# Chunk pairs of the modulated input padded by 32 bytes, in a two-layer decoder trunk

## The chip, the cores and the metric

The kernel runs on one core of a Trainium2 chip. The metric is the time of one execution on the device, in microseconds; less is better. The time before is the median of three executions.

## What is computed

Two layers of a decoder over one sequence of 256 tokens with 2048 features, in f32. Layer 0 mixes tokens with a forgetting attention of 16 heads, layer 1 with a sliding-window attention of 32 query heads; each mixer is followed by a gated feed-forward network whose up-projection passes a causal convolution of width 3. Cut to what matters:

```python
for i in range(DEPTH):                                   # DEPTH = 2
    sh1, sc1, g1, sh2, sc2, g2 = split(silu(c) @ ada_w[i] + ada_b[i], 6)
    h = x * (1 + sc1) + sh1
    y = fox_attention(h, ...) if i == 0 else swa_attention(h, ...)
    x = layer_norm(ALPHA * x + (1 + g1) * y)
    h = x * (1 + sc2) + sh2
    u = causal_conv3(h @ w_up)                           # 2048 -> 2 * 5632
    y = (silu(u[..., :5632]) * u[..., 5632:]) @ w_down
    x = layer_norm(ALPHA * x + (1 + g2) * y)
```

## The kernel before, in words

**Split products.** Every large product runs as float32r matmuls on operands that are split into a high and a low part. A weight tile `w` of 128 partitions x 2 x 512 comes by DMA from SyncE's queue. `stream` has ScalarE copy its high part into `wh` (L264) and VectorE put the rest into `wl` (L275). Of each product, the terms high x high, high x low and low x high are added in PSUM.

**The modulated input.** `h = x * (1 + scale) + shift`, transposed, stands in one tile `hHL`: 16 chunks of 128 features, each with 256 f32 numbers of the high part (`hH`) and then 256 of the low part (`hL`), 2048 bytes a chunk in each partition. `mod_pair` writes two chunks at a time.

**Who multiplies it.** Four kinds of product read the operands; all matmuls are issued through the helper at L75, so the profile tells them apart by tiles. The operand named as stationary is put into the array by a weight load, a separate instruction; the moving one streams through.

- `u_mm`, tile `us`, the up-projections: a piece of `wh` is stationary, and `hH` and `hL` together stream as 512 columns; then a piece of `wl` is stationary and `hH` streams as 256 columns.
- `w_mm`, tile `ws`, the query and key projections of layer 0: the same operands in three matmuls of 256 columns.
- `x_mm` with `hstat`, tile `xs<-..,hHL`: a piece of `hHL` is stationary and 512 columns of `wh` or `wl` stream. The value projections of layer 0, all projections into layer 1's attention, and the last four of the 16 chunks of both output projections, whose attention output `o_tile` puts into `hHL`.
- `x_mm` with `gT` or `oT`: the same with stationary pieces in buffers of the pool `gp` (down-projections, the other 12 chunks of the output projections).

**Order.** `stream` puts weight tiles into a list, `settle` takes them off it; attention heads, evictions and the adaLN vectors are generators that advance between tiles. The adaLN weights come by the same queue, and VectorE multiplies and adds them (L404).

**Where the tiles lie.** In each partition `hHL` begins at byte 27,904, the four buffers of `wh` at 119,776 and every 4096 on, those of `wl` at 136,160, those of the pool `gp` at 152,544 and every 2048 on. Pieces of `wh`, `wl`, `gT`, `oT` and `hHL` that a weight load reads are 512 bytes long and begin at multiples of 512 from these. So every moving operand lies at one offset from every stationary one, modulo 512 bytes: `hHL` lies 288 behind the weights' pieces where it moves, the weights lie 224 behind `hHL`'s pieces where `hHL` is stationary (512 - 288), and 0 behind pieces in `gp`. The last tile ends at byte 229,280 of 229,376, so there are 96 bytes to spare; the first 4096 are a scratch for DMAs that GpSimd issues (biases, the convolution's weights, the `ada_b` rows).

Of the kernel before, what the change touches and what calls it, by code (L numbers as in the profile page):

```python
# [11 lines left out]
F32R = mybir.dt.float32r  # L12
# [5 lines left out]
P = 128  # L18
D = 2048
S = 256  # L20
NT = S // P
KC = D // P
# [19 lines left out]
def hybrid_trunk(ctx: ExitStack, tc: tile.TileContext, a: dict, out: bass.AP):  # L42
    nc = tc.nc
# [4 lines left out]
    cst = ctx.enter_context(tc.tile_pool(name="cst", bufs=1))  # L48
# [431 lines left out]
            ada_step()  # L480


    hHL = cst.tile([P, KC, 2, S], F32R, name="hHL")
    hH, hL = hHL[:, :, 0, :], hHL[:, :, 1, :]

    def mod_turn(k, n=1):

# [670 lines left out]
    for t in range(NT):  # L1158
        mu, rs, _ = moments[t]
        for d in range(D // 512):  # L1160
            c = slice(d * 512, (d + 1) * 512)
# [29 lines left out]
```

## Time and profile before

| what | us |
|---|---|
| median of three executions | 2254.76 (2251.33 to 2254.91) |
| the profiled execution, its own time | 2256.46 |
| its span, first to last instruction | 2254.7 |
| TensorE matmuls busy | 2203.7 (98%) |
| weight loads busy | 1908.6 (85%) |
| VectorE busy | 1847.5 (82%) |
| ScalarE busy | 1209.7 (54%) |
| GpSimd busy | 22.8 (1%) |
| 5632 matmuls `us`, busy | 983.7 + 790.4 |

Matmuls overlap in the trace: one starts while the one before is still shown as running. So the sum of their durations is not the time they take; that is read from the distance between starts. A weight load is shown beside the matmul before the one that it is for.

### The profile page before, as it was taken

To read this page: it belongs to the slowest core of one execution; us is meant where nothing else is said; L and a number is where in the kernel's file an instruction comes from. 1 tells how busy PE (TensorE), PEld (TensorE's weight loads), DVE (VectorE), ACT (ScalarE), POOL (GpSimd) and SP (SyncE) were. 2 spreads that over 40 slices of the span, in tenths; PEclk is the share of its full clock that TensorE was granted. 3 is DMA by queue.
4 is the path that set the end of the run, shared out by engine and by line. 5 is a ranking of instruction groups with operands and counts; after the bars stand their busy time and mean duration, and the time that the engine had idled before them with its cause. 6 is when DMAs were issued, how large, how long until landed. Compare 5 with 4: busy or idle time off the path is not lost. (4 is left out here: it accounts for less than half of the span.)

```text
span 2254.7 us, 33120 instructions
## 1 busy us (share of the span) xinstructions
PE 2203.7 (98%) x12087; PEld 1908.6 (85%) x12087; DVE 1847.5 (82%) x2626; ACT 1209.7 (54%) x2009; POOL 22.8 (1%) x52
## 2 busy tenths in 40 slices
PE   6999999999999999999999999999999999999997
PEld 5999888788888888888887788788888888888886
DVE  6879999979989978799888899769988655676766
ACT  3435655455555543655634588746555533555542
POOL 0000000000000000000000000000000000000000
PEclk9999999999999999999999999999999999999999
DMA  9999999958978989889887777557887555565553
GB/s 336 371 336 364 349 357 325 329 200 298 327 266 296 315 299 339 272 277 319 280 309 284 244 246 243 206 185 262 289 270 256 190 192 195 189 193 189 188 195 112
DMA packets 274228, 602.66 MB, mean 267 GB/s; under 512 B 21062, under 2 KB 29960, under 8 KB 273552
## 3 DMA queue, kind: packets, MB, share of 16 engines
q1 hardware_dynamic: 273008, 595.85, 76.5%
q0 software_dynamic: 1056, 4.69, 0.6%
q8 instruction: 94, 1.54, 0.3%
q14 instruction: 70, 0.57, 0.1%
HBM read 598.37 MB, written 2.10 MB: 266 GB/s over the span
## 5 line engine op out<-in xcount | busy, mean ns | idle before, releaser
L264 ACT CAST wh<-w 128x1024 fp32r<-128x1024 f32 x728 | 763.8, 1051 | 806.4 <-PE us L75 284.5
L275 DVE TENSOR_TENSOR wl<-w,wh 128x1024 fp32r<-128x1024 f32 x728 | 887.2, 1223 | 297.0 <-ACT wh L264 285.1
L75 PE MATMUL us<-hHL,wh 128*128 128x512 f32 x2816 | 983.7, 393 | 0.0
L75 PE MATMUL us<-hHL,wl 128*128 128x256 f32 x2816 | 790.4, 282 | 3.0 <-DVE wl L275 3.0
L75 PEld LDWEIGHTS us<-hHL,wh 128*128 128x128 f32 x2816 | 528.9, 188 | 112.0 <-issue 2.5
L75 PEld LDWEIGHTS us<-hHL,wl 128*128 128x128 f32 x2816 | 533.0, 189 | 8.4 <-DVE wl L275 4.3
L75 PE MATMUL xs<-wh,gT 128*128 128x512 f32 x1408 | 435.5, 390 | 0.0
L75 PEld LDWEIGHTS xs<-wh,gT 128*128 128x128 f32 x1408 | 264.3, 188 | 54.6
L75 PE MATMUL xs<-wl,gT 128*128 128x512 f32 x704 | 273.9, 389 | 0.0
L75 PE MATMUL xs<-wh,hHL 128*128 128x512 f32 x704 | 237.6, 403 | 0.1
L404 DVE SCALAR_TENSOR_TENSOR acc<-wa,cact,acc 128x1024 f32<-128x1024 f32 x180 | 228.8, 1280 | 0.0
L75 PE MATMUL ws<-hHL,wh 128*128 128x256 f32 x1024 | 191.3, 289 | 4.4 <-ACT hHL L84 2.1
L75 PEld LDWEIGHTS ws<-hHL,wh 128*128 128x128 f32 x1024 | 163.1, 196 | 6.9 <-ACT hHL L84 2.3
L404 DVE SCALAR_TENSOR_TENSOR acc<-wa,cactp,acc 128x1024 f32<-128x1024 f32 x128 | 162.6, 1281 | 0.0
L75 PEld LDWEIGHTS xs<-wh,hHL 128*128 128x128 f32 x704 | 131.5, 189 | 29.4 <-issue 1.0
L75 PEld LDWEIGHTS xs<-wl,gT 128*128 128x128 f32 x704 | 132.2, 188 | 27.3
L75 PE MATMUL ws<-hHL,wl 128*128 128x256 f32 x512 | 144.7, 290 | 2.2 <-DVE wl L275 2.2
L75 PE MATMUL xs<-wl,hHL 128*128 128x512 f32 x352 | 140.6, 400 | 1.6 <-DVE wl L275 1.5
L75 PE MATMUL xs<-wh,oT 128*128 128x512 f32 x384 | 124.6, 394 | 0.8 <-ACT wh L264 0.7
L1075 ACT ACTIVATE u<-us,ccol 128x256 f32<-128x256 f32 x176 | 98.0, 561 | 39.6 <-DVE us L1073 39.5
L75 PEld LDWEIGHTS ws<-hHL,wl 128*128 128x128 f32 x512 | 99.5, 197 | 2.8 <-DVE wl L275 2.8
L1076 DVE SCALAR_TENSOR_TENSOR u<-us,ccol,u 128x255 f32<-128x255 f32 x176 | 83.6, 480 | 13.2 <-ACT u L1075 12.9
(222 smaller groups left out, 1761.2 us busy)
## 6 DMA issues: line engine op xcount, KB each, us to landing
w<-in_ffn_w_up_dram SPq DMA_DIRECT2D x352, 512.0 KB, 4.6
wa<-in_ada_w_dram SPq DMA_DIRECT2D x320, 512.0 KB, 5.4
w<-in_ffn_w_down_dram SPq DMA_DIRECT2D x176, 512.0 KB, 4.1
w<-in_fox_w_in_dram SPq DMA_DIRECT2D x96, 512.0 KB, 7.0
wo<-in_ada_w_dram SPq DMA_DIRECT2D x48, 512.0 KB, 8.4
w<-in_swa_w_in_dram SPq DMA_DIRECT2D x40, 512.0 KB, 5.0
w<-in_fox_w_o_dram SPq DMA_DIRECT2D x32, 512.0 KB, 6.2
w<-in_swa_w_o_dram SPq DMA_DIRECT2D x32, 512.0 KB, 4.7
```

Of the source, the lines that this page charges most:

```text
L75: return nc.tensor.matmul(o, lhsT, rhs, start=start, stop=stop, **kw)
L264: pin(nc.scalar.copy(h, w), False)
L275: pin(nc.vector.tensor_tensor(l, w, f32(h), op=ALU.subtract), behind[0] > 0)
L404: pin(nc.vector.scalar_tensor_tensor(ac, wo, (cactp if row else cact)[:, k:k + 1], ac, op0=ALU.mult, op1=ALU.add), True)
L1075: nc.scalar.activation(u, pf, AF.Identity, bias=cw(CW, f), scale=cw(2, f))
L1076: nc.vector.scalar_tensor_tensor(u[:, 1:], pf[:, :S - 1], cw(1, f), u[:, 1:], op0=ALU.mult, op1=ALU.add)
```

## The change

The tile `hHL` becomes eight chunk pairs of 4 x 256 numbers with 8 unused numbers (32 bytes) behind each, 256 bytes longer in all. A class `Chunks` stands for the former three views and finds pair and chunk. The scratch of dynamic transfers is 2048 instead of 4096 bytes per partition, without which the longer tile would not fit.

```diff
-    hHL = cst.tile([P, KC, 2, S], F32R, name="hHL")
-    hH, hL = hHL[:, :, 0, :], hHL[:, :, 1, :]
+    hpad = cst.tile([P, KC // 2, 4 * S + 8], F32R, name="hHL")[:, :, :4 * S].rearrange("p j (i a s) -> p j i a s", i=2, a=2)
+
+    class Chunks:
+
+        def __init__(self, a):
+            self.a = a
+
+        def __getitem__(self, key):
+            _, k, *c = key
+            j, i = (k.start // 2, slice(0, 2)) if isinstance(k, slice) else (k // 2, k % 2)
+            return hpad[(slice(None), j, i, self.a, *c)]
+
+    hHL, hH, hL = Chunks(slice(0, 2)), Chunks(0), Chunks(1)
...
-    nc = _bacc.Bacc("TRN2", target_bir_lowering=False, num_devices=1, dynamic_dma_scratch_size=4096)
+    nc = _bacc.Bacc("TRN2", target_bir_lowering=False, num_devices=1, dynamic_dma_scratch_size=2048)
```

On each of the five engines the instructions stand in the same order as before, with the same shapes and the same waits; what differs is addresses. Tiles up to `hHL`'s start move down by 2048 bytes, those behind it by 1792. With j the number of the chunk pair, 0 to 7, `hHL` as moving operand now lies 32 + 32j bytes behind the weights' pieces modulo 512 (32, 64, ... 256, where it was 288), and the weights as moving operand lie 512 - 32 - 32j behind `hHL`'s pieces (480, 448, ... 256, where it was 224). Against pieces in `gp` they stay at 0.

## The prediction

> **What bounds the kernel now.** I read the page first. Its engine and clock rows say that TensorE is the bound nearly throughout:
>
> ```profile
> span 2254.7 us, 33120 instructions
> PE 2203.7 (98%) x12087; PEld 1908.6 (85%) x12087; DVE 1847.5 (82%) x2626; ACT 1209.7 (54%) x2009; POOL 22.8 (1%) x52
> PEclk9999999999999999999999999999999999999999
> ```
>
> The groups say which matmuls carry it, and that they hardly wait: the last column is idle time ahead of a group, and it is at most a few us in a thousand.
>
> ```profile
> L75 PE MATMUL us<-hHL,wh 128*128 128x512 f32 x2816 | 983.7, 393 | 0.0
> L75 PE MATMUL us<-hHL,wl 128*128 128x256 f32 x2816 | 790.4, 282 | 3.0 <-DVE wl L275 3.0
> L75 PE MATMUL xs<-wh,hHL 128*128 128x512 f32 x704 | 237.6, 403 | 0.1
> L75 PE MATMUL xs<-wl,hHL 128*128 128x512 f32 x352 | 140.6, 400 | 1.6 <-DVE wl L275 1.5
> L75 PE MATMUL ws<-hHL,wh 128*128 128x256 f32 x1024 | 191.3, 289 | 4.4 <-ACT hHL L84 2.1 <-ACT wh L264 1.3 <-ACT hHL L503 1.0
> L75 PE MATMUL ws<-hHL,wl 128*128 128x256 f32 x512 | 144.7, 290 | 2.2 <-DVE wl L275 2.2
> ```
>
> So 2816 pairs of `us`, 704 + 352 = 1056 `xs` with `hHL` stationary and 1024 + 512 = 1536 `ws` touch the tile that changes. Since nothing is added, removed or reordered, only the pace of these matmuls can change, and the pace is the distance between starts. I therefore read the timeline, TensorE alone, in stretches without a break.
>
> ```profile
> 1455.24 0.39 PE L75 MATMUL xs<-wl,oT 128*128 128x512 f32 x1
> ...
> 1469.52 0.39 PE L75 MATMUL xs<-wl,oT 128*128 128x512 f32 x1
> 1469.75 0.40 PE L75 MATMUL xs<-wh,oT 128*128 128x512 f32 x1
> 1469.98 0.39 PE L75 MATMUL xs<-wh,hHL 128*128 128x512 f32 x1
> 1470.21 0.39 PE L75 MATMUL xs<-wl,hHL 128*128 128x512 f32 x1
> 1470.44 0.63 PE L75 MATMUL xs<-wh,hHL 128*128 128x512 f32 x2
> ...
> 1475.11 0.40 PE L75 MATMUL xs<-wl,hHL 128*128 128x512 f32 x1
> 1475.34 0.40 PE L75 MATMUL xs<-wh,hHL 128*128 128x512 f32 x1
> 1475.58 0.39 PE L75 MATMUL xs<-wh,oT 128*128 128x512 f32 x1
> ```
>
> This is one output projection that goes over from stationary pieces in `gp` to pieces in `hHL` and back. The moving operand, the length and the engines around it are the same; only the address of the loaded piece differs. From 1455.24 to 1469.52 there are 21 rounds of three matmuls, 14.28/63 = 226.7 ns each. From 1470.21 to 1475.11 there are 7 rounds, 4.90/21 = 233.3 ns. So where the weight load reads relative to the stream costs 6.6 ns a matmul here: offset 0 is a cheap place, offset 224 a dear one. The two other kinds:
>
> ```profile
> 286.92 0.28 PE L75 MATMUL ws<-hHL,wl 128*128 128x256 f32 x1
> 287.04 0.40 PE L75 MATMUL ws<-hHL,wh 128*128 128x256 f32 x2
> ...
> 289.37 0.28 PE L75 MATMUL ws<-hHL,wl 128*128 128x256 f32 x1
> 599.70 0.39 PE L75 MATMUL us<-hHL,wh 128*128 128x512 f32 x1
> 599.93 0.28 PE L75 MATMUL us<-hHL,wl 128*128 128x256 f32 x1
> ...
> 605.94 0.39 PE L75 MATMUL us<-hHL,wh 128*128 128x512 f32 x1
> ```
>
> `ws`: 7 rounds of three, 2.45/21 = 116.7 ns for 256 columns. `us`: 18 pairs, 6.24/18 = 346.7 ns a pair. Both lie at offset 288. A pair at the cheapest rows would take 226.7 + 116.7 = 343.4. For a dear pair I take 233.3 and, for the 256 columns that no row shows dear, 116.7 plus half of 6.6, together 353.3. The pair now stands a third of the way from the cheap to the dear end.
>
> **The Trainium skill against this.** TensorE: Matmul & The Clock Gate, section Step-by-step: what each phase is for, says that the array has two independent read ports, and that "Loading the next tile's weights doesn't steal SBUF read bandwidth from the running matmul." By that rule the sum would be zero; the trace does not agree, 226.7 against 233.3 ns with only the loaded piece's address changed. The same page, section Back-to-back issue gap, gives 512/2.4 + 2.5 = 216 ns for 512 columns and 109 for 256; an estimate by it is that a change which took all interference away would save 2816 x (347 - 325) = 62 us in `us` alone, and no row here reaches that pace in these products.
>
> **The change part by part.** The cost of a load is taken as a function of the offset, moving minus stationary, modulo 512. The rows give it at 0 (cheap), 224 (dear) and 288 (a third of the way). For a new offset I take the nearest of these; that is a choice, because three points don't show a curve.
>
> *us.* The new offsets are 32, 64, ... 256 for the eight chunk pairs, each with an eighth of the matmuls. 32, 64 and 96 lie nearest to 0; I take no gain there, because no 256-column row is cheaper than now (bound: 343.4, a gain of 3.3). 128, 160, 192 and 224 lie nearest to 224: +6.6 each. 256 lies midway between 224 and 288: +3.3. Mean (4 x 6.6 + 3.3)/8 = 3.7 ns, times 2816: **+10.5 us**. Bounds: all cheap, -9.3; all dear, +18.6.
>
> *xs with hHL.* 480, 448 and 416 lie nearest to 512, that is 0: -6.6. 384, 352, 320 and 288 lie nearest to 288, a third of the way up: -4.4. 256 is midway: -2.2. Mean -(19.8 + 17.6 + 2.2)/8 = -5.0 ns, times 1056: **-5.3 us**. Bounds -7.0 and 0.
>
> *ws.* +3.3 at four offsets and +1.7 at one, mean 1.9 ns, times 1536 = 2.9 us. This stage has a second bound beside TensorE:
>
> ```profile
> 200.00:300.00 100.00, 97.12 (x728) 91.10 (x728) 92.44 (x144) 59.08 (x127) 5.85 (x12) 1.00 0.98 346
> 600.00:640.00 40.00, 40.00 (x233) 35.48 (x232) 38.72 (x55) 23.41 (x36) 0.00 (x0) 1.00 0.91 321
> 1950.00:2000.00 50.00, 50.00 (x291) 44.34 (x290) 34.75 (x53) 28.30 (x46) 0.00 (x0) 1.00 0.60 190
> ```
>
> These are stretches with the busy time of PE, PEld, DVE, ACT and POOL, granted clock, DMA share and GB/s. With DMA at 0.98 the queues take part of what TensorE loses, so I count half: **+1.4 us** (bounds 0 and +5.1). In the up-projections TensorE is busy all the time in both layers (40.00 of 40, 50.00 of 50), so there a loss counts in full; a gain in layer 0 would soon meet VectorE, 38.72 of 40 busy, which is what would be late next.
>
> *The padding itself.* Chunks are written by the same instructions with the same shapes, so nothing is taken for it; a slower write would be hidden behind the matmuls of the pair before.
>
> *The scratch.* GpSimd issues few transfers, and is idle 99% of the time. One is not far from the path: an `ada_b` row issued between the two moments of a layer norm.
>
> ```profile
> 472.28 0.57 POOL L642 TENSOR_TENSOR rs<-mv,mhalf 128x1 f32<-128x1 f32 x1 [211.50 <-DVE mv L641]
> 476.09 0.60 POOL L392 DMA_DIRECT2D acc<-in_ada_b_dram  x1 [3.24 <-PE sm L75]
> 476.71 0.57 POOL L642 TENSOR_TENSOR rs<-mv,mhalf 128x1 f32<-128x1 f32 x1
> acc<-in_ada_b_dram POOLq DMA_DIRECT2D x4, 1024.0 KB, 6.2
> ```
>
> Issuing takes 0.60 us of GpSimd. If it still fits into the scratch, it costs nothing.
>
> **The sum.** 10.5 - 5.3 + 1.4 = +6.6 us. The profiled execution took 2256.46 us, of which 2254.7 is span; it would take 2263.1. The median of the runs lies 1.7 us below that execution, so the forecast is 2254.76 + 6.6 = 2261 us. About 0.2%, 4.5 us, is what a measurement of this kernel can tell from no change.
>
> **The rivals.**
>
> *Alignment decides, not distance (faster).* The bytes modulo 64 may be what matters. The weights and the buffers of `gp` begin 32 bytes past a multiple of 64, `hHL` at a multiple: every cheap row has both operands in the same place, every other row has them 32 apart. The padding puts the four odd chunk pairs where the weights are. Then half of `xs` falls to 226.7, 528 x 6.6 = 3.5 us, and half of the `us` pairs to 343.4, 1408 x 3.3 = 4.6 us; `ws` stays. Together -8.1 us: 2247. For it speaks that it, too, explains all rows; against it that `ws` at 116.7 and `us` at 346.7 hardly show the handicap that `xs` shows. It decides from the point where fewer than about a third of the `us` loads become dear. A stronger form has every new offset cheap: -9.3 - 7.0 = -16.3, 2238.
>
> *Nothing happens (same).* While a load reads its 512 bytes, the stream runs on over more bytes than that, so that every offset modulo 512 could be met in every load, and 226.7 against 233.3 would come from something else in the place of `hHL`. Then the pace stays: 2255. This is also where the rule of the two ports ends. Against it: the pace is constant over long stretches, and differs by tile alone.
>
> *All new offsets are dear (slower still).* +18.6 + 5.1 = 23.7: 2278.
>
> *The scratch is too small (slower).* If half of it doesn't hold the descriptors of an `ada_b` row, GpSimd waits in L392 until part of the transfer has landed, with the second `rs` (L642) queued behind it; the normalisation and TensorE wait for that. Price: up to the 6.2 us of a landing, at the one layer norm shown and the like one of layer 1: up to 12 us, 2267 without any change of pace. For it speaks only the place; GpSimd had issued nothing for 200 us before.
>
> **How the numbers follow.** The forecast has 0.38, all dear 0.08, the scratch 0.03: slower 0.49. Nothing happens: same 0.18. Alignment 0.25 and all cheap 0.08: faster 0.33. The three points don't fix a curve, which is why the forecast has less than half. The range must take in both ends of the unknown curve, 2238 and 2278, with some us for what the runs scatter: 2236 to 2282.
>
> **What the profile after would show.** If I am right, the `us` pairs have two paces that change with the chunk pair: about 347 ns in the pairs 0 to 2, about 353 in the pairs 3 to 6; `xs` with `hHL` falls to 227 to 229 except in the last pair; `oT` and `gT` stay at 226.7; L392 stays at 0.6 us. Alternating cheap and dear pairs, even against odd, would speak for alignment. One pace of 346.7 in all pairs would say that the offset modulo 512 is not the cause. A `us` pace under 343 anywhere would say that my cheap end is not the end.

## The result, and the profile after

The median went from 2254.84 us (four runs, 2251.33 to 2255.42) to 2265.36 us (four runs, 2262.47 to 2265.58): 10.5 us slower, ratio 1.0047 with a 95% interval of 1.003 to 1.0064. The forecast was 6.6 us slower, 2261.

The page of the changed kernel, the rows that answer to those of before:

```profile
span 2263.2 us, 33120 instructions
PE 2212.6 (98%) x12087; PEld 1906.7 (84%) x12087; DVE 1848.3 (82%) x2626; ACT 1210.4 (53%) x2009; POOL 22.9 (1%) x52
L75 PE MATMUL us<-hHL,wh 128*128 128x512 f32 x2816 | 993.8, 397 | 0.0
L75 PE MATMUL us<-hHL,wl 128*128 128x256 f32 x2816 | 787.6, 281 | 2.9 <-DVE wl L275 2.9
L75 PE MATMUL xs<-wh,hHL 128*128 128x512 f32 x704 | 236.1, 401 | 0.1
L75 PE MATMUL ws<-hHL,wh 128*128 128x256 f32 x1024 | 192.7, 290 | 4.4 <-ACT hHL L84 2.1
```

The same instructions, no new wait, and the idle column as small as before. TensorE alone is longer busy, by 8.9 us, while VectorE and ScalarE stay within a microsecond. The group that grew is `us` beside `wh`, by 10.1 us.

Where it lies shows in the timeline of TensorE. These are the first matmuls of each chunk pair in one undisturbed up-projection (columns: start, duration, both in us). Between one row and the next stand eight `us` pairs:

```profile
1961.46 0.40 PE L75 MATMUL us<-hHL,wh 128*128 128x512 f32 x1
...
1964.24 0.39 PE L75 MATMUL us<-hHL,wh 128*128 128x512 f32 x1
...
1967.04 0.40 PE L75 MATMUL us<-hHL,wh 128*128 128x512 f32 x1
...
1969.84 0.39 PE L75 MATMUL us<-hHL,wh 128*128 128x512 f32 x1
...
1972.65 0.40 PE L75 MATMUL us<-hHL,wh 128*128 128x512 f32 x1
...
1975.43 0.39 PE L75 MATMUL us<-hHL,wh 128*128 128x512 f32 x1
...
1978.25 0.39 PE L75 MATMUL us<-hHL,wh 128*128 128x512 f32 x1
...
1981.06 0.39 PE L75 MATMUL us<-hHL,wh 128*128 128x512 f32 x1
...
1983.89 0.40 PE L75 MATMUL us<-hHL,wh 128*128 128x512 f32 x1
```

Before, every pair took 346.6 ns in the median, whatever its chunk. Now each chunk pair has a pace of its own, and keeps it from block to block. The medians over some 40 passes of each chunk pair, worked out from all starts of the trace, are 347.8, 350.5, 350.1, 350.4, 347.9, 352.2, 351.6 and 353.5 ns for the pairs 0 to 7. Their mean is 350.5, so 3.9 ns more, times 2816 pairs: 10.9 us. All eight are slower than before.

`xs` with `hHL` stationary, the last four chunks of an output projection, 24 matmuls:

```profile
1493.63 0.39 PE L75 MATMUL xs<-wh,hHL 128*128 128x512 f32 x1
...
1498.98 0.39 PE L75 MATMUL xs<-wh,hHL 128*128 128x512 f32 x1
```

5.35/23 = 232.6 ns, against 233.0 before (5.36 us for the like 23 from 1469.98 to 1475.34): hardly the fall that was forecast. The same four chunks for the 512 output columns before these fall further:

```profile
1471.79 0.39 PE L75 MATMUL xs<-wh,hHL 128*128 128x512 f32 x1
...
1477.08 0.39 PE L75 MATMUL xs<-wh,hHL 128*128 128x512 f32 x1
```

5.29/23 = 230.0 ns. Both stretches have the same offsets; what differs is the order of their matmuls.

### The profile page after: what moved, and what is told of

The parts are those of the page before. It is cut to its first block, busy times and chain, and to the rows that moved or that the text cites. A ratio compares the mean times of both kernels' runs of the same rounds, so it can differ in the third digit from the quotient of the medians.

```text
span 2263.2 us, 33120 instructions
## 1 busy us (share of the span) xinstructions
PE 2212.6 (98%) x12087; PEld 1906.7 (84%) x12087; DVE 1848.3 (82%) x2626; ACT 1210.4 (53%) x2009; POOL 22.9 (1%) x52
## 5 line engine op out<-in xcount | busy, mean ns | idle before, releaser
L75 PE MATMUL us<-hHL,wh 128*128 128x512 f32 x2816 | 993.8, 397 | 0.0
```

Source lines behind the costliest of these rows:

```text
L75: return nc.tensor.matmul(o, lhsT, rhs, start=start, stop=stop, **kw)
```

## The experiments

Each run is compared with runs of the kernel before on the same chip. "Halved" is the kernel before with the scratch of 2048 bytes; offsets are the moving operand's place behind the loaded piece.

**1. The scratch alone.**

```diff
-    nc = _bacc.Bacc(..., dynamic_dma_scratch_size=4096)
+    nc = _bacc.Bacc(..., dynamic_dma_scratch_size=2048)
```

> The kernel before with half the scratch alone: all tiles move down by 2048 bytes, no offset between operands changes (hHL 288 behind the weights everywhere). Theory (the pace of a matmul follows from the offset of the moving operand to the piece being loaded, modulo 512 bytes): no change, 2254.8 us within 2, us pairs at 346.7 ns. Rival, the scratch or the absolute place of the tiles costs the time: some 10 us more, 2265, and L392 on GpSimd longer than 0.6 us.

2254.92 against 2254.53 us, ratio 1.0008 (0.9999 to 1.0017): no change. GpSimd's issue of an `ada_b` row stands between the two `rs` as before and takes as long:

```profile
473.74 0.60 POOL L392 DMA_DIRECT2D acc<-in_ada_b_dram  x1 [3.24 <-PE sm L75]
474.36 0.57 POOL L642 TENSOR_TENSOR rs<-mv,mhalf 128x1 f32<-128x1 f32 x1
```

So neither the scratch nor the move of all tiles costs anything that these runs can see.

**2. Padding that changes no offset.** The changed kernel, with a longer pad:

```diff
-    hpad = cst.tile([P, KC // 2, 4 * S + 8], F32R, name="hHL")...
+    hpad = cst.tile([P, KC // 2, 4 * S + 64], F32R, name="hHL")...
```

> The changed kernel with 256 instead of 32 unused bytes behind each chunk pair: the same class of views, the same half scratch, chunk pairs still apart, but every pair 32 behind the weights modulo 256, as in the kernel before. Theory: the whole loss goes, 2255 within 3, us pairs at 346.5 ns, xs with hHL at 233. Rival, the padding or the scratch costs in itself, whatever the offsets: 2265.

2254.78 against 2256.36 us, ratio 0.9993 (0.9983 to 1.0003): the whole loss is gone, with the pads, the views and the small scratch still there. A whole up-projection block, 64 pairs:

```profile
1976.24 0.39 PE L75 MATMUL us<-hHL,wh 128*128 128x512 f32 x1
...
1998.42 0.39 PE L75 MATMUL us<-hHL,wh 128*128 128x512 f32 x1
```

22.18/64 = 346.6 ns, one pace. The offsets are the cause, not the padding.

**3. One offset for all chunks, 32 and 256.** The halved kernel with 256, or 32, unused bytes behind the old tile:

```diff
-    hHL = cst.tile([P, KC, 2, S], F32R, name="hHL")
+    hHL = cst.tile([P, KC * 2 * S + n], F32R, name="hHL")[:, :KC * 2 * S].rearrange(...)   # n = 64 or 8
```

> The old layout of hHL with 256 unused bytes behind it: hHL lies 32 behind the weights in all chunks, as chunk pair 0 of the changed kernel does. Theory: the pace of that pair everywhere, about 347 ns a us pair, 233 an xs with hHL: 2816 x 0.5 = 1.4 us more, 2256. Rival, the mixture of offsets costs (going from one to the next): as before, 2255, so this run alone does not part the two; rival, the shift of the weights by 1792 instead of 2048 bytes: 2265.

> The old layout with 32 unused bytes behind it: 256 behind in all chunks, as chunk pair 7 of the changed kernel, and the weights at a multiple of 64 bytes as hHL is. Theory: the pace of pair 7 everywhere, about 352 ns a us pair (+5.4 x 2816 = 15 us), 228.3 an xs with hHL (-5 x 1056 = -5 us), ws 121 (+4.5 x 1536 = 7, some of it hidden): 2269 to 2272, more than the changed kernel. Rival, the mixture costs: 2255. Rival, equal alignment modulo 64 is what makes it cheap: 2247 or less.

Offset 32: 2254.01 against 2254.53, ratio 0.9996 (0.9988 to 1.0005), the pace of before (median 346.6 ns; pair 0 of the changed kernel, at the same offset beside others, has 347.8). It also clears the shift of the weights by 1792 bytes. Offset 256: 2264.69 against 2254.53, ratio 1.0048 (1.0035 to 1.006). One uniform dear offset loses as much as the mixture of eight; a mixture is not needed. The alignment rival, by which this run should have been the fastest, falls. The expected 2269 to 2272 was too high. Over distances between starts below 300 ns (longer ones hold a wait or other work), `us` cost 13.0 us where 15 were expected, and `ws` 2.3 where 7 were, some of it hidden. Why `us` fell short is in the trace. Two blocks of 64 pairs of the same kernel:

```profile
597.58 0.39 PE L75 MATMUL us<-hHL,wh 128*128 128x512 f32 x1
...
619.77 0.39 PE L75 MATMUL us<-hHL,wh 128*128 128x512 f32 x1
...
1982.03 0.40 PE L75 MATMUL us<-hHL,wh 128*128 128x512 f32 x1
...
2004.64 0.40 PE L75 MATMUL us<-hHL,wh 128*128 128x512 f32 x1
```

22.19/64 = 346.7 ns in the first half of layer 0's up-projection, 22.61/64 = 353.3 in layer 1, at the same offsets. At this offset there are two paces; the trace stays in one for some 200 us at a time, and the changes that were followed up lie where other matmuls come between. `xs` with `hHL` gains here:

```profile
1491.66 0.39 PE L75 MATMUL xs<-wh,hHL 128*128 128x512 f32 x1
...
1496.87 0.40 PE L75 MATMUL xs<-wh,hHL 128*128 128x512 f32 x1
```

5.21/23 = 226.5 ns, the pace that `gT` has at offset 0. So modulo 256 one and the same offset, 0, is cheap for `xs` and dear for `us`, as 32 is cheap for `us` and dear for `xs` (233.1 ns in pair 6 of the changed kernel).

The run also speaks against the place of a tile by itself, without the other operand. The weights and `gp` begin 32 bytes further on here, modulo 256, than in the changed kernel. Yet that kernel's pair 7, at the same offset as all pairs here, has 353.5 ns against the 353.3 above, and `gT`, moved together with the weights, keeps its 226.8 ns.

**4. The other half of the circle.** The changed kernel with 256 unused bytes more behind the tile:

```diff
-    hpad = cst.tile([P, KC // 2, 4 * S + 8], ...)[:, :, :4 * S]...
+    hpad = cst.tile([P, KC // 2 * (4 * S + 8) + 64], ...)[:, :KC // 2 * (4 * S + 8)]...
```

> The changed kernel with 256 more unused bytes behind hHL, so that the eight chunk pairs lie 288, 320, ... 512 behind the weights: the other half of the circle. Theory: pair 0 (288) has the pace of before, 346.7 ns in us and 233 in xs with hHL; pair 7 (512, that is 0) has 226.7 in xs; the pairs between have paces of their own, from 343 to 353, not those of the changed kernel. Sum between 2245 and 2270. Rival, the mixture costs: 2265, with the same paces as in the changed kernel pair by pair.

2264.26 against 2254.53, ratio 1.0048 (1.0034 to 1.0062). The paces are those of the changed kernel, chunk pair by chunk pair: 347.8, 350.5, 350.1, 350.4, 347.9, 352.2, 351.6 and 353.5 ns as medians. The last pair, offset 512:

```profile
2001.26 0.39 PE L75 MATMUL us<-hHL,wh 128*128 128x512 f32 x1
...
2004.09 0.40 PE L75 MATMUL us<-hHL,wh 128*128 128x512 f32 x1
```

2.83/8 = 353.8, as pair 7 at offset 256 in the changed kernel (2.83/8). Here the mixture rival expected the right paces and the theory the wrong ones. Read with the two runs before, which exclude the mixture as the cause, it says that the offset counts modulo 256: 288 is 32, 512 is 256. The run of 2 agrees: its pairs lie at 288 and 32 in turn, and all have one pace.

**5. Other tiles at the dear place.** The halved kernel with 32 unused bytes ahead of the pool `gp`:

```diff
             l = hl.tile([P, 2, WB], F32R, tag="wl", name="wl")
+            hl.tile([P, 8], F32, tag="gap", bufs=1, name="gap")
```

> The layout of before with the pool gp (gT, oT) moved by 32 bytes: wh and wl, where they stream, lie 224 instead of 0 behind the pieces in gp, the place that hHL's pieces had; hHL and the weights stay as they were. Theory (offset modulo 256 between stream and loaded pieces, whatever the tiles): xs with gT goes from 226.6 to 233 ns, with oT alike, us stays at 346.5; (2112 + 576) x 6.5 = 17 us more, 2271. Rival, hHL is dear for a reason of its own (its place, who writes it): 2254.

2268.96 against 2256.23, ratio 1.0058 (1.0042 to 1.0075). The down-projections, which the change never touched, go from the first of these stretches (before) to the second, 576 matmuls in a row each:

```profile
1779.92 0.39 PE L75 MATMUL xs<-wh,gT 128*128 128x512 f32 x1
...
1910.27 0.39 PE L75 MATMUL xs<-wh,gT 128*128 128x512 f32 x1
```

```profile
1785.76 0.40 PE L75 MATMUL xs<-wh,gT 128*128 128x512 f32 x1
...
1919.92 0.40 PE L75 MATMUL xs<-wh,gT 128*128 128x512 f32 x1
```

130.35/575 = 226.7 ns became 134.16/575 = 233.3, the pace of `hHL`'s pieces to a tenth. So nothing about `hHL` itself is dear; the offset is. The loss was 12.7 us, not 17. By distances below 300 ns, `gT` lost 13.7 us and `oT` 2.9, together what was expected; the time shows 4 us less than that, and why was not followed up.

**6. Which piece counts.** As in 5, with a gap of 32 bytes ahead of `wl` instead, and 224 behind it, so that `hHL` lies 32 behind `wh` and 0 behind `wl`, modulo 256:

> The layout of before, but the buffers of wl moved by 32 bytes against those of wh (and the pool gp put back to 0 behind wh). So hHL lies 32 behind wh and 0 behind wl. Theory, what counts is the piece loaded while a matmul streams: the 512 columns of us, beside which wl is loaded, go from 228 to 234 ns, the 256 columns, beside which wh is loaded, stay at 118; 2816 x 4 to 6 = 11 to 17 us; where wl streams beside a load of gT (704) some 6 ns more, 4 us; together 2268 to 2276. Rival, what counts is the piece already in the array: the 512 columns stay at 228 and the 256 columns fall to 116 or 117, 3 to 6 us less in us, 4 more in gT: 2250 to 2256.

2266.82 against 2253.5, ratio 1.0057 (1.004 to 1.0074). The time is just under what the first reading expected (2268 to 2276), but for another reason. The `us` pairs don't slow down (first fence, 64 pairs: 22.19/64 = 346.7 ns), and `gT` slows down as a whole, though only `wl`, a third of the streams, changed its place (576 matmuls, 134.15/575 = 233.3):

```profile
1961.90 0.39 PE L75 MATMUL us<-hHL,wh 128*128 128x512 f32 x1
...
1984.09 0.39 PE L75 MATMUL us<-hHL,wh 128*128 128x512 f32 x1
```

```profile
1783.14 0.39 PE L75 MATMUL xs<-wh,gT 128*128 128x512 f32 x1
...
1917.29 0.39 PE L75 MATMUL xs<-wh,gT 128*128 128x512 f32 x1
```

Both readings fall: the first on `us`, the second on `gT`. A matmul's pace doesn't follow from its own stream and one piece; neighbours take part. The `us` pairs even gain in parts of this run, at the same offsets; a block of 64 pairs in layer 1's first half:

```profile
1597.53 0.39 PE L75 MATMUL us<-hHL,wh 128*128 128x512 f32 x1
...
1619.58 0.39 PE L75 MATMUL us<-hHL,wh 128*128 128x512 f32 x1
```

22.05/64 = 344.5 ns, so here too there are two paces. In all, `us` gains 2.1 us by distances below 300 ns.

**7. The order of the streams.** The kernel of 6, and the halved kernel as control, with `x_mm` in another order:

```diff
             for i in range(2):
                 xh, xl = stat(kc + i, t)
                 mm(ps[t], xh, h[:, i, :], start=kc + i == first)
-                mm(ps[t], xh, l[:, i, :])
-                mm(ps[t], xl, h[:, i, :], stop=kc + i == last)
+                mm(ps[t], xl, h[:, i, :])
+            for i in range(2):
+                mm(ps[t], stat(kc + i, t)[0], l[:, i, :], stop=kc + i == last)
```

> The run with wl moved by 32 bytes, with the matmuls of x_mm in another order: of two chunks first the four that stream wh, then the two that stream wl, so that the stream goes over from wh to wl and back once in six matmuls instead of twice. There all three matmuls of a round with gT had become slower (231 to 236 ns for 226.6), though only wl's stream had changed its place. If the going over from one offset to another is what costs: about half of the 13.6 us that gT lost, xs with gT at some 230 ns, 2260. If a third of the streams at a dear place sets the pace of all: no difference from that run, 233 ns, 2266. If each stream pays for itself (which that run spoke against): the same sum, with the four wh at 226.6.

> The control to the run before it: the same order of x_mm with wl in its old place. Both readings: xs with gT at 226.6 ns, 2254.

Each ran once: 2265.66 and 2257.5 us. In the first, the stretch with `gT` takes 132.67/574 = 231.1 ns:

```profile
1784.55 1.09 PE L75 MATMUL xs<-wh,gT 128*128 128x512 f32 x4
...
1917.22 0.63 PE L75 MATMUL xs<-wl,gT 128*128 128x512 f32 x2
```

The control stays at 226.7 by the starts of its trace. With half as many changes from one stream to the other, two thirds of the loss remain (4.4 of 6.6 ns). That is between the two readings and settles neither. How one matmul bears on the next stays open.

**8. Finer steps.** The changed kernel moved by 16 bytes, and one with 2 instead of 8 numbers of padding (8 bytes) from offset 0 on; each ran once. Offsets are modulo 256.

> The changed kernel with all of hHL moved by 16 bytes: the eight chunk pairs lie at 48, 80, ... 240 and 16 behind the weights modulo 256, between the offsets seen so far. Theory: each pair has a pace of its own between 343 and 353 ns in us; near the changed kernel's time, 2260 to 2268. If whole multiples of 32 are what matters (a word that straddles a line), all pairs are dearer than any seen, over 352.

> Padding of 8 bytes a chunk pair: the pairs lie at 0, 8, ... 56 behind the weights modulo 256. Theory: pair 0 at about 351 ns in us and pair 4 (32) at about 347, as seen at these offsets, and the others between; tells whether there is a place cheaper than 32 near it. If only the 16-byte line counts, pairs 0 and 1 agree, 2 and 3, and so on.

2263.12 and 2265.03 us. Offsets 48, 80, ... 240 and 16 have medians from 347.9 to 352.0 ns a pair, so whole multiples of 32 are nothing special. In steps of 8 bytes from 0 the medians are 353.0, 353.6, 348.4, 356.8, 347.2, 348.4, 346.5 and 347.0. The first matmuls of the pairs at 16, 24 and 32, eight `us` pairs apart:

```profile
1966.69 0.40 PE L75 MATMUL us<-hHL,wh 128*128 128x512 f32 x1
...
1969.47 0.39 PE L75 MATMUL us<-hHL,wh 128*128 128x512 f32 x1
...
1972.33 0.39 PE L75 MATMUL us<-hHL,wh 128*128 128x512 f32 x1
```

2.78/8 = 347.5 ns at 16 and 2.86/8 = 357.5 at 24. Places 8 bytes apart differ by 8 to 10 ns here, which speaks against 16 bytes as the unit. In these two runs no place is cheaper than 346.5, and 24 bytes is the dearest seen. But the offset does not fix a pace to the nanosecond: 48 has 349.0 in the first run and 346.5 in the second, between other neighbours.

**9. A version from what was learnt.** Two views of one tile, 32 bytes apart, so that `hHL` lies at 32 where it moves and at 0 where it is stationary (layer 1's projections, the output projections):

```diff
+    hraw = cst.tile([P, KC * 2 * S + 8], F32R, name="hHL")
+    hviews = [hraw[:, o:o + KC * 2 * S].rearrange("p (k a s) -> p k a s", a=2, s=S) for o in (0, 8)]
...
```

> One tile with 32 bytes more and two views of it, 32 bytes apart: where hHL moves (us, ws) and for layer 0's value projection it lies 32 behind the weights modulo 256, the cheap place of before; for layer 1's projections and the four chunks of both output projections that are stationary pieces in hHL, it lies at 0, where the run with 256 for all showed xs at 228.5 ns instead of 233. Theory (an offset modulo 256 for each kind of product): 672 x 4.4 = 3 us less than before, 2251.5, us pairs at 346.5 as before. Rival, the pace of xs in that run came from something else than its own offset: 2254.5.

2251.94 against 2253.5, ratio 0.9994 (0.9984 to 1.0004). The pace is what was expected, 24 matmuls of an output projection:

```profile
1485.68 0.39 PE L75 MATMUL xs<-wh,hHL 128*128 128x512 f32 x1
...
1490.89 0.40 PE L75 MATMUL xs<-wh,hHL 128*128 128x512 f32 x1
```

5.21/23 = 226.5 ns for 233, and the `us` pairs keep theirs. By distances below 300 ns `xs` with `hHL` gains 3.0 us in all, as expected. The gain of 1.6 us in the time, against 3 expected, is inside what the runs scatter, so this version is not shown to be faster than the kernel before.

## Why the prediction was right, and where not

**The bound.** TensorE's pace was the only thing that changed: same instructions, no new wait, and it stayed busy throughout in the up-projections (50.00 of the 50 us from 1950 to 2000, before and after).

**us.** Forecast +10.5 us, measured 2816 x 3.9 = +10.9 by the medians. The sum was right and its parts were not. The pairs 0 to 2 were to stay at 347 and the pairs 3 to 6 to go to 353; in fact the pairs 1 and 2 lost 3.9 and 3.5 ns, pair 4 only 1.3, and pair 7, taken at half, lost most, 6.9. The nearest of three rows is no guide to a curve that jumps within 8 bytes, and two of the three rows were those of `xs`, which has another curve: offset 0, its cheap place, is a dear one for `us`. What carried the sum was one observation: `us` stood near its cheap end, so that most other places had to be dearer. The finer runs bear it out: in them no place is cheaper than 346.5. That wrong parts came to the sum within half a us is luck.

**xs with hHL.** Forecast -5.3 us, which is 5.0 ns a matmul. Over distances below 300 ns the mean went from 233.2 to 232.0 ns, so -1.3 us. The step that failed is the offset modulo 512. It counts modulo 256, so 480 is 224, the dear row itself, where the forecast took it for near 0; and 256 is 0. The five projections of layer 1 show it, with means over each chunk pair: 233.4, 233.3 and 233.6 ns in the pairs 0 to 2, which were to fall most; 229.9 in pair 5 and 229.1 in pair 7; 232.2 to 233.1 in the others.

**ws.** Forecast +1.4 us after halving; by the same distances 124.1 and 125.2 ns, +1.6 us. But in runs that leave the offset of `ws` as it was, this mean lies between 122.1 (run of 9) and 124.3 (run of 1), so that the term is not clear of what the stage scatters.

**The sum.** By the same distances `us` has +10.4, and all three +10.4 - 1.3 + 1.6 = +10.7, against 10.5 in the medians and 8.5 in the two spans. The forecast of 6.6 fell short mostly by the gain of `xs` that did not come. So the direction and the bearer of the loss were read rightly from the profile, the places that bear it were not.

**The rivals.** Alignment modulo 64 is excluded by the run at 256. The scratch is excluded by its own run. That nothing happens is excluded by the result, and that all new offsets are dear, 2278, by the time and by pairs such as 0 and 4 (347.8 and 347.9 ns). The rule in the Trainium skill that "nothing happens" rested on (TensorE: Matmul & The Clock Gate, section Step-by-step: what each phase is for) has two read ports, so that a load takes nothing from the running stream. The trace does not agree: moving one pool by 32 bytes took `gT` from 226.7 to 233.3 ns. That the weight load is the other party is the likely reading. It is argued, not shown, since no run here streams without loads.

## What to carry to other kernels

When an engine is busy all the time and nothing waits, compare distances between starts of equal instructions on different tiles; a few ns that differ by tile alone may be an address effect and can be tried with a pad. A layout that happens to stand at a good offset can lose by being spread over many, and the good offset need not be the same for each kind of product; so change one offset for all, and undo it with a pad that leaves the offset alone. Moving any tile of a full memory moves all tiles behind it, and with them offsets in products that the change never meant.

## What the runs showed of the hardware that was not expected

- The pace of these float32r matmuls, each with a load of its own, depends on the offset of stream and piece modulo 256 bytes, with jumps between places 8 bytes apart (348.4 to 356.8 ns a pair). Two different layouts 256 bytes apart gave the same eight paces. Offset 0 was cheap for 512 columns of weights over pieces of `hHL` (226.5 ns) and dear for the `us` pairs (353.3 in one of their two paces).
- At one offset there can be two paces, 346.7 and 353.3 ns a pair in the same execution, each held for some 200 us at a time.
- A third of the streams at another offset made all matmuls of a round dear (226.7 to 233.3 ns).
